# Making the rotations of eight scan steps ahead of the scan and keeping them in DRAM

## The chip, the core and the metric

The kernel runs on one core of one Trainium2 chip. Five engines take part, each with an instruction queue of its own that is worked off in order: TensorE (PE, matrix products), VectorE (DVE), ScalarE (ACT), GpSimd (POOL) and SyncE (SP, which here issues every DMA). Data move between DRAM and the on-chip memory SBUF on sixteen DMA engines. The metric is the device time of one execution in microseconds (us); lower is better.

## What is computed

Two streams (a prompt of 128 tokens and a sample of 1024, width 1024) go through two layers, each a mixer followed by an MLP, all in fp32 accuracy. What matters here is the mixer of layer 0. Three quarters of its channels go through a diagonal state-space scan (S5) in both directions, the rest through a Fourier mixer:

```python
def s5_direction(u, h0_re, h0_im, lam_re, lam_im, log_dt, b_re, b_im, c_re, c_im):
    ab_re, ab_im, bb_re, bb_im = s5_discretize(lam_re, lam_im, log_dt, b_re, b_im)
    bu_re = jnp.einsum("blgh,gph->blgp", u, bb_re)
    bu_im = jnp.einsum("blgh,gph->blgp", u, bb_im)
    ...
    _, _, h_re, h_im = lax.associative_scan(_complex_linear_combine, (a_re, a_im, bu_re, bu_im), axis=1)
    y = jnp.einsum("blgp,ghp->blgh", h_re, c_re) - jnp.einsum("blgp,ghp->blgh", h_im, c_im)
    return y, h_re[:, -1], h_im[:, -1]

def even_mixer(h, ...):
    z = h @ w_in
    ya, s_re, s_im = s5_mixer(z[..., :S5_CH], ...)
    yb = fnet_mixer(z[..., S5_CH:], fnet_w, fnet_b)
    return jnp.concatenate([ya, yb], axis=-1) @ w_out, (s_re, s_im)
```

Each layer also needs six modulation vectors: `silu(cond) @ w_mod + b_mod`, cut in twelve chunks of 512 columns.

## The kernel before

A product in fp32 accuracy is made of three matmuls on split operands (`mm3`, `wh` and `wl` being the high and low part of a weight). A scheduler of the tile framework sets the order of instructions on each engine from a simulated timeline, except in the very first stage, where the order on SP is the order in which the code is written.

**Mixer's products.** The function `layer0_scan` first norms and transposes the tokens and then forms z = h @ w_in in 24 blocks (`z_block`: six blocks of 128 channels, three groups of tokens each). After each second block, from the fourth on, it calls `tables(hb, ...)`, which through `s5_tables` makes the two matrices of one scan step, `et` and `f` (together the tile `ef`), and a small matrix `xd`. A table costs VectorE fourteen operations (L1532 to L1551, L1572), PE some transposes and small products (`pet`, `px`), ScalarE a few copies and GpSimd two sums of 64 columns (`bs` at L1525, `cs` at L1526) and a fill (`bd`, L1555). Tables are kept in SBUF for steps 0 and 1 and stored to DRAM for the others. The list of early steps is 2 to 9, then 0 and 1, ten in all, but the calls come eleven times: the first takes index -1 of the list, so the table of step 1 is made twice. The tables of steps 10 and 11 are made in the scan.

**Scan.** Twelve steps (`hb`), each for 64 channels in both directions. `s5_inputs_of` loads the inputs `u` of a step and makes its rotations `rt`, the powers of a unit complex number for 146 chunks: two complex products of tables of 15 and 9 entries, that is two times L1608, two times L1609 (128 partitions x 540 elements each) and four times L1611 (270 each), on VectorE for step 0 and on GpSimd for all others, and two ScalarE copies (L1613, L1614). `s5_scan` then has eight operations on VectorE: twice `rotated` (two of L1666 on 1168 elements each, with `rt` read), L1669 and L1670, two scans L1673, L1677 and L1678. PE makes its input (`pv`) and output (`py`). Beside the steps nineteen jobs are put: nine of the Fourier mixer ("f") and ten of the modulation ("m"), in the order of the string `JSEQ`. A modulation job loads four pieces of 512 KB (`mst`), has PE multiply them (`pmod`, L127, 16 instructions), and turns the row into columns (`pmc`, `pmg`) with three small VectorE operations (L143 to L146).

**After the scan.** `glu` (products `pg`) follows, then the product with w_out (`mixer_out`), and the MLP's upward half `ff_up` in 16 pairs of weight blocks (`pair`). The ten modulation jobs that the scan did not take are put behind the first ten pairs, one each (`K.late`). Line numbers here are those of the kernel before.

Of the kernel before, what the change touches and what calls it, by code (L numbers as in the profile page):

```python
# [9 lines left out]
F32 = mybir.dt.float32  # L10
# [3 lines left out]
AF = mybir.ActivationFunctionType  # L14
ALU = mybir.AluOpType
# [9 lines left out]
NQ = 48  # L25
SC = 146
UC = 147
YC = 145
EARLY = 10
JSEQ = "ffffmmfffffmmmmmmmm"  # L30
AHA = (3, 7)
TB = 3
RW = 152
# [45 lines left out]
def ap_of(t, off, dims):  # L79

    return bass.AP(tensor=t.tensor, offset=t.offset + off, ap=[list(t.ap[0])] + [list(d) for d in dims])


def load_unit(K, src, n=1024, tags=("wh", "wl")):

    nc = K.nc
    st = stage_tile(K)
    nc.sync.dma_start(st[:, :n], src)
    wh = K.whp.tile([128, 1024], FR, name="wh", tag=tags[0])
    wl = K.wlp.tile([128, 1024], FR, name="wl", tag=tags[1])  # L90
    nc.scalar.activation(wh[:, :n], st[:, :n], AF.Copy)  # L91
    nc.vector.tensor_tensor(wl[:, :n], st[:, :n], wh[:, :n].bitcast(F32), op=ALU.subtract)  # L92
    return wh, wl
# [8 lines left out]
def bank(K, name, tags=None):  # L102

    tags = tags or K.bank_tags
    tag, bufs = tags[K.turn % len(tags)]
    K.turn += 1
    return K.psum.tile([128, 512], F32, name=name, tag=tag, bufs=bufs)
# [132 lines left out]
def mm_cm(K, g, act, w, ps, kbs=range(8)):  # L240

    ah, al = act
    wh, wl = w
    for kb in kbs:
        s = slice(128 * kb, 128 * kb + 128)
        mm3(K.nc, ps[:, :G], wh[:, s], wl[:, s], ah[kb], al[kb], kb == 0, kb == 7)
# [14 lines left out]
def build(tc, A):  # L261
# [6 lines left out]
    with ExitStack() as top:  # L268
# [27 lines left out]
        K.wlp = top.enter_context(tc.tile_pool(name="wlp", bufs=4, reuse_waits="tile"))  # L296
        K.mod = [{}, {}]
        gd, yd = layer0_scan(K)
        K.psum = top.enter_context(tc.tile_pool(name="psum", bufs=1, space=PSUM, reuse_waits="tile"))
        K.bank_tags, K.side_tags = [("s0", 1), ("s1", 1), ("s2", 1)], [("t", 2)]  # L300
# [14 lines left out]
def layer0_scan(K):  # L315

    tc, nc, A = K.tc, K.nc, K.A
    v = nc.vector
    with ExitStack() as ph:
# [10 lines left out]
        with ExitStack() as pa:  # L330
# [86 lines left out]
            s5t = ph.enter_context(tc.tile_pool(name="s5t", bufs=1, reuse_waits="tile"))  # L417
# [3 lines left out]
            S = K.S5  # L421
# [3 lines left out]
            def tables(hb, pool, keep):  # L425
                ef = pool.tile([128, 2176], F32, name="ef", tag="ef", bufs=2 if pool is s5t else 1)
                s5_tables(K, s5t, hb, ef)
                if keep:
                    efs[hb] = ef
                else:  # L430
                    spill[hb] = tc.dram_tile([128, 2176], F32, name=f"ef{hb}")
                    nc.sync.dma_start(spill[hb], ef)

            early = list(range(2, EARLY)) + [0, 1]
            with tc.tile_pool(name="zt", bufs=2, side="right", reuse_waits="tile") as ztp:
                zts = {}
                done = [0]

                def z_block(b, g, w, ps=None):
                    if ps is None:  # L440
                        ps = bank(K, "pz")
                        mm_cm(K, g, acts[g], w, ps)
                    if b >= 6:
                        nc.scalar.activation(zbs[b - 6][:, G * g:G * g + G], ps[:, :G], AF.Copy)
                    else:
                        z_part(b, g, ps)
                    done[0] += 1
                    if done[0] >= 24 - 2 * len(early) and done[0] % 2 == 0:
                        hb = early[(done[0] - 24 + 2 * len(early)) // 2 - 1]
                        tables(hb, s5t, hb < 2)  # L450

                def z_part(b, g, ps):
                    if g == 0:
                        zts[b] = ztp.tile([128, 8 * YC], F32, name="zt", tag="zt")
                        nc.gpsimd.memset(zts[b].rearrange("p (r c) -> p r c", c=YC)[:, :, 128:129], 0.0)
                    zv = zts[b].rearrange("p (r c) -> p r c", c=YC)
                    n = 3 if g < 2 else 2
                    nc.scalar.activation(zv[:, 3 * g:3 * g + n, :128],
                                         ps[:, :128 * n].rearrange("p (r c) -> p r c", c=128), AF.Copy)
                    if g == 2:  # L460
                        nc.scalar.activation(zv[:, :, 129:],
                                             ps[:, 256:384].rearrange("p (r c) -> p r c", c=16), AF.Copy)
                        nc.sync.dma_start(zd[b], zts[b])

                for g in range(3):
                    ps = [bank(K, "pz") for _ in range(4)]
                    for kb in range(8):
                        for wb, p in zip(w, ps):
                            mm_cm(K, g, acts[g], wb, p, (kb,))
                    with tc.high_priority():  # L470
                        for b, p in zip(first, ps):
                            z_block(b, g, None, p)
                for b in range(2, 6):
                    wb = load_unit(K, A["w_in0"][b])
                    for g in range(3):
                        z_block(b, g, wb)
# [3 lines left out]
        with tc.tile_pool(name="s5", bufs=1, side="right", reuse_waits="tile") as s5:  # L480
# [3 lines left out]
                                (1, "sc2", 4, "g_ff_pre"), (1, "sh2", 3, None), (1, "gt2", 5, "g_ff_post")))  # L484
            jobs = [(dft if x == "f" else mods).pop(0) for x in JSEQ]
            K.late = dft + mods
            order = [s5, s5t, s5t]

            def inputs(hb):
                W = s5_inputs_of(K, s5, hb, zd[hb // 2])  # L490
                if hb not in efs:
                    pool = order[(hb + 1) % 3]
                    if hb in spill:
                        efs[hb] = pool.tile([128, 2176], F32, name="ef", tag="ef", bufs=2 if pool is s5t else 1)
                        nc.sync.dma_start(efs[hb], spill[hb])
                    else:
                        tables(hb, pool, True)
                W.m = s5_toeplitz(K, s5, hb)
                W.et, W.f = ef_views(efs[hb])
                return W  # L500
# [1083 lines left out]
def s5_inputs_of(K, pool, hb, zd):  # L1584


    nc, S = K.nc, K.S5
    gp = nc.gpsimd
    q0 = 4 * hb
    e = hb % 2  # L1590
    W = Ctx()

    def T(shape, name, bufs):
        return pool.tile(shape, F32, name=name, tag=name, bufs=bufs)

    W.u = u = T([128, 4, UC], "u", 2)
    gp.memset(u[:, :, 0:1], 0.0)
    gp.memset(u[:, :, 146:147], 0.0)
    for g in range(4):
        r0 = 64 * e + 16 * g  # L1600
        nc.sync.dma_start(u[:, g, 1:146], zd[r0:r0 + 16].rearrange("h (r c) -> r h c", c=YC))
    rt = T([128, 2, 4, RW], "rt", 2)
    t1, t2 = (T([128, 4, 15, 9], n, 1) for n in ("rtmp1", "rtmp2"))
    a = [ap_of(S.rr, 24 * (NQ * ri + q0), [(24, 4), (1, 15), (0, 9)]) for ri in range(2)]
    b = [ap_of(S.rr, 24 * (NQ * ri + q0) + 15, [(24, 4), (0, 15), (1, 9)]) for ri in range(2)]
    eng = nc.vector if hb == 0 else gp
    for ri, op in ((0, ALU.subtract), (1, ALU.add)):
        eng.tensor_tensor(t1, a[0], b[ri], op=ALU.mult)  # L1608
        eng.tensor_tensor(t2, a[1], b[1 - ri], op=ALU.mult)  # L1609
        for d in range(2):  # L1610
            eng.tensor_tensor(ap_of(rt, 4 * RW * ri + d * (2 * RW + 17), [(RW, 2), (9, 15), (1, 9)]),  # L1611
                             t1[:, 2 * d:2 * d + 2], t2[:, 2 * d:2 * d + 2], op=op)
    nc.scalar.activation(rt[:, :, 0:2, 129:146], rt[:, :, 0:2, 0:17], AF.Copy)  # L1613
    nc.scalar.activation(rt[:, :, 2:4, 0:17], rt[:, :, 2:4, 17:34], AF.Copy)  # L1614
    W.R = rt[:, :, :, 0:SC]
    W.rho = rho = T([128, 4, SC], "rho", 1)
    for q in range(4):
        nc.scalar.activation(rho[:, q], K.cst[:, 144 + SC * (q // 2):144 + SC * (q // 2 + 1)], AF.Copy,
                             scale=S.rho[:, q0 + q:q0 + q + 1])
    return W  # L1620


def s5_toeplitz(K, pool, hb):
# [240 lines left out]
```

## Time and profile before

| | us |
|---|---|
| median of 3 runs | 2401.62 (2399.34 to 2403.82) |
| the profiled execution, its own time | 2401.66 |
| its span, first to last instruction | 2399.9 |
| PE busy in the span | 2261.0 (94%) |
| DVE busy | 1695.4 (71%) |
| ACT busy | 980.8 (41%) |
| POOL busy | 190.9 (8%) |

The shares are means over stages that differ. The mixer's products with the tables run from about 84 to 190 us of the span, the scan from 200 to 408, glu and w_out to about 600, the first `ff_up` from about 640 to 1000. All of GpSimd's arithmetic lies before 480. The profiled execution takes 1.8 us outside its span.

### The profile page before, as it was taken

Reading aid. Unit: us, or ns where it says so; the run is one execution under the profiler, and the core shown is the slowest. Engines: PE = TensorE matmul, PEld = TensorE weight load, DVE = VectorE, ACT = ScalarE, POOL = GpSimd, SP = SyncE. Lnnn points to the kernel's source line nnn. Section 1 sums busy time; section 2 is a strip of 40 time slices with the busy share of each in tenths; the row PEclk is TensorE's granted clock in tenths of the full one; section 3 lists DMA queues with packets and bytes.
Section 4 is the critical chain, followed back from the end, with each engine's and each line's share of the span. In section 5 each row is a group of like instructions: output and inputs, shape, how many; then the busy total and the mean of one; then the engine's idle time right before and its main releaser. Section 6 shows DMA issues by size and latency. Waiting matters only on the chain.

```text
span 2399.9 us, 34805 instructions
## 1 busy us (share of the span) xinstructions
PE 2261.0 (94%) x13462; PEld 1974.3 (82%) x13462; DVE 1695.4 (71%) x2694; ACT 980.8 (41%) x1694; POOL 190.9 (8%) x197
## 2 busy tenths in 40 slices
PE   7997676998999999999999899998899999999997
PEld 4996544987888899988888699887899999888886
DVE  7888998747755555757777844867766566677778
ACT  4533324646423233443343452446333333533332
POOL 0127773200000000000000000000000000000000
PEclk9998888999999999999999899998999999999999
DMA  8375675322556553745343431132344446544433
GB/s 308 135 260 170 198 247 154 139 85 91 165 186 204 175 192 123 251 149 157 109 150 98 147 113 36 62 114 79 115 152 129 130 147 219 178 124 137 145 107 141
DMA packets 200453, 361.48 MB, mean 151 GB/s; under 512 B 50064, under 2 KB 95760, under 8 KB 198240
## 3 DMA queue, kind: packets, MB, share of 16 engines
q1 hardware_dynamic: 200288, 359.26, 45.6%
q8 instruction: 106, 1.74, 0.3%
q14 instruction: 59, 0.48, 0.1%
HBM read 256.69 MB, written 102.51 MB: 150 GB/s over the span
## 4 chain that ended last, share of the span: by engine, by line
PE 80%; DVE 13%; DMA 2%; ACT 2%; issue 2%; POOL 1%; SPq 0%; DVEq 0%; ACTq 0%
PE pz L1170 8%; PE pz L1172 8%; PE pz L1173 8%; PE puA L97 6%; PE puA L98 5%; PE puA L99 5%; DVE tp L1666 3%; PE puC L97 3%; PE puC L98 3%; PE puC L99 3%; PE po L256 3%; PE po L257 3%; PE po L258 3%; PE pmod L127 2%; DVE xp L1673 1%
## 5 line engine op out<-in xcount | busy, mean ns | idle before, releaser
L1170 PE MATMUL pz<-wh,hh 128*128 128x512 f32 x840 | 326.2, 389 | 1.2 <-DVE z L1184 1.2
L1173 PE MATMUL pz<-wh,hl 128*128 128x512 f32 x840 | 327.0, 389 | 0.0
L1172 PE MATMUL pz<-wl,hh 128*128 128x512 f32 x840 | 326.9, 389 | 0.0
L1158 ACT ACTIVATE hh<-hr 128x1024 fp32r<-128x1024 f32 x96 | 96.7, 1007 | 262.3 <-PE pz L1172 233.1
L1170 PEld LDWEIGHTS pz<-wh,hh 128*128 128x128 f32 x840 | 157.7, 188 | 34.7 <-issue 2.0
L1173 PEld LDWEIGHTS pz<-wh,hl 128*128 128x128 f32 x840 | 157.7, 188 | 32.7
L1172 PEld LDWEIGHTS pz<-wl,hh 128*128 128x128 f32 x840 | 157.7, 188 | 32.6
L1159 DVE TENSOR_TENSOR hl<-hr,hh 128x1024 fp32r<-128x1024 f32 x96 | 110.9, 1155 | 91.4 <-ACT hh L1158 91.4
L1184 DVE TENSOR_TENSOR z<-z,pz 128x512 f32<-128x512 f32 x192 | 122.8, 681 | 31.8 <-PE pz L1173 31.1
L877 ACT ACTIVATE wh<-c 128x512 fp32r<-128x512 f32 x96 | 60.6, 631 | 186.4 <-DVE c L886 134.3
L933 DVE TENSOR_TENSOR h<-puA,c 128x576 f32<-128x576 f32 (+1 forms) x34 | 24.5, 722 | 155.1 <-PE puA L99 152.0
L257 PE MATMUL po<-wl,act 128*128 128x512 f32 x288 | 113.2, 393 | 0.0
L258 PE MATMUL po<-wh,act 128*128 128x512 f32 x288 | 112.7, 393 | 0.0
L256 PE MATMUL po<-wh,act 128*128 128x512 f32 x288 | 112.3, 395 | 0.0
L878 DVE TENSOR_TENSOR wl<-c,wh 128x512 fp32r<-128x512 f32 x96 | 66.0, 687 | 34.2 <-ACT wh L877 33.8
L877 ACT ACTIVATE wh<-st 128x512 fp32r<-128x512 f32 x96 | 57.1, 627 | 74.8 <-PE puB L98 29.1
L1666 DVE TENSOR_TENSOR tp<-rt,xp 128x1168 f32<-128x1168 f32 x48 | 81.1, 1727 | 7.3 <-ACT xp L1659 6.7
L1134 DVE TENSOR_TENSOR wl<-raw,wh 128x1024 fp32r<-128x1024 f32 (+1 forms) x64 | 73.1, 1153 | 18.2 <-ACT wh L1133 18.2
L92 DVE TENSOR_TENSOR wl<-st,wh 128x1024 fp32r<-128x1024 f32 (+1 forms) x42 | 52.1, 1251 | 47.3 <-ACT wh L91 47.3
L878 DVE TENSOR_TENSOR wl<-st,wh 128x512 fp32r<-128x512 f32 x96 | 63.5, 685 | 29.2 <-ACT wh L877 29.2
L929 ACT ACTIVATE c<-puA 128x576 f32<-128x576 f32 (+1 forms) x68 | 42.2, 621 | 90.0 <-PE puA L99 89.0
L127 PE MATMUL pmod<-mst,csil 128*32 128x512 f32 x384 | 75.9, 659 | 1.0 <-DMA mst<-in_w_mod_dram 1.0
(492 smaller groups left out, 6747.9 us busy)
## 6 DMA issues: line engine op xcount, KB each, us to landing
hr<-hd SPq DMA_DIRECT2D x102, 512.0 KB
mst<-in_w_mod_dram SPq DMA_DIRECT2D x96, 512.0 KB
st<-in_w_ff_dram SPq DMA_DIRECT2D x68, 512.0 KB
hd<-hsum SPq DMA_DIRECT2D x120, 256.0 KB
raw<-in_w_ff_dram SPq DMA_DIRECT2D x56, 512.0 KB
hd<-h SPq DMA_DIRECT2D x98, 256.0 KB
ef<-ef SPq DMA_DIRECT2D x16, 1088.0 KB
xr<-xs SPq DMA_DIRECT2D x32, 512.0 KB
```

The lines of the kernel that those rows point to most:

```text
L97: nc.tensor.matmul(ps, sh, mh, start=start, stop=False, skip_group_check=shared)
L98: nc.tensor.matmul(ps, sh, ml, start=False, stop=False, skip_group_check=shared)
L99: nc.tensor.matmul(ps, sl, mh, start=False, stop=stop, skip_group_check=shared)
L127: nc.tensor.matmul(ps[32 * j:32 * j + 32, :], K.csil[:, kb, :], st[:, 512 * k:512 * k + 512], start=kb < 4, stop=kb >= 4, skip_group_check ...
L256: K.nc.tensor.matmul(ps, ah[kb][:, c], wh[:, s], start=kb == 0, stop=False)
L257: K.nc.tensor.matmul(ps, ah[kb][:, c], wl[:, s], start=False, stop=False)
L258: K.nc.tensor.matmul(ps, al[kb][:, c], wh[:, s], start=False, stop=kb == 7)
L878: v.tensor_tensor(wl, x, wh.bitcast(F32), op=ALU.subtract)
L1170: nc.tensor.matmul(o, hh[:, q, t], wh[:, q], start=start and s == 0 and q == 0, stop=False, skip_group_check=True)
L1172: nc.tensor.matmul(o, hh[:, q, t], wl[:, q], start=False, stop=False, skip_group_check=True)
L1173: nc.tensor.matmul(o, hl[:, q, t], wh[:, q], start=False, stop=s == 1 and q == n - 1, skip_group_check=True)
L1666: v.tensor_tensor(t[:, k], R[:, k:k + 1].to_broadcast([128, 2, 4, SC]), x, op=ALU.mult)
```

## The change

The rotations of steps 0 to 7 (`TURNS = 8`) are made in the stage of the mixer's products, one set after each of the first eight tables, all on GpSimd, into one tile `rt` of a pool with one buffer; ScalarE makes the two copies; SP stores the set to DRAM (`rt0` to `rt7`, 598 KB each, in rows of 584 bytes on the SBUF side). In the scan, `s5_inputs_of` loads the stored set for these steps; for steps 8 to 11 GpSimd makes it there as before. The early list now has eleven steps (2 to 10, then 0 and 1) and the index is mended, so eleven calls make eleven tables; only the table of step 11 is left for the scan. `JSEQ` has three more "m": the scan takes thirteen modulation jobs, and `ff_up` has seven left. The three are both halves of the layer's last gate (`gt2`) and the first half of the next layer's first.

```diff
-EARLY = 10
-JSEQ = "ffffmmfffffmmmmmmmm"
+EARLY = 11
+TURNS = 8
+JSEQ = "ffffmmmfffffmmmmmmmmmm"
...
-            with tc.tile_pool(name="zt", bufs=2, side="right", reuse_waits="tile") as ztp:
+            S.rd = {}
+            with tc.tile_pool(name="zt", bufs=2, side="right", reuse_waits="tile") as ztp, \
+                    tc.tile_pool(name="rtz", bufs=1, side="right", reuse_waits="tile") as rtp:
...
-                    if done[0] >= 24 - 2 * len(early) and done[0] % 2 == 0:
-                        hb = early[(done[0] - 24 + 2 * len(early)) // 2 - 1]
-                        tables(hb, s5t, hb < 2)
+                    n = (done[0] - 24) // 2 + len(early) - 1
+                    if n >= 0 and done[0] % 2 == 0:
+                        tables(early[n], s5t, early[n] < 2)
+                        if n < TURNS:
+                            rt = rtp.tile([128, 2, 4, RW], F32, name="rt", tag="rt")
+                            s5_rotations(K, rt, [rtp.tile([128, 4, 15, 9], F32, name=x, tag=x) for x in ("rt1", "rt2")], n)
+                            S.rd[n] = tc.dram_tile([128, 2, 4, SC], F32, name=f"rt{n}")
+                            nc.sync.dma_start(S.rd[n], rt[:, :, :, 0:SC])
...
-    eng = nc.vector if hb == 0 else gp
-    for ri, op in ((0, ALU.subtract), (1, ALU.add)):
-        eng.tensor_tensor(t1, a[0], b[ri], op=ALU.mult)
...
+    if hb in S.rd:
+        nc.sync.dma_start(rt[:, :, :, 0:SC], S.rd[hb])
+    else:
+        s5_rotations(K, rt, [T([128, 4, 15, 9], n, 1) for n in ("rtmp1", "rtmp2")], hb)
...
+def s5_rotations(K, rt, tmp, hb):
+    nc, S = K.nc, K.S5
+    gp = nc.gpsimd
+    q0 = 4 * hb
+    t1, t2 = tmp
...
+    for ri, op in ((0, ALU.subtract), (1, ALU.add)):
+        gp.tensor_tensor(t1, a[0], b[ri], op=ALU.mult)
+        gp.tensor_tensor(t2, a[1], b[1 - ri], op=ALU.mult)
+        for d in range(2):
+            gp.tensor_tensor(ap_of(rt, 4 * RW * ri + d * (2 * RW + 17), [(RW, 2), (9, 15), (1, 9)]),
+                             t1[:, 2 * d:2 * d + 2], t2[:, 2 * d:2 * d + 2], op=op)
+    nc.scalar.activation(rt[:, :, 0:2, 129:146], rt[:, :, 0:2, 0:17], AF.Copy)
+    nc.scalar.activation(rt[:, :, 2:4, 0:17], rt[:, :, 2:4, 17:34], AF.Copy)
```

What stands in a row on GpSimd, in the stage of the mixer's products, from the second table to the fourth, before the change:

```order
L1525 TENSOR_TENSOR bs<-s5bb 128x64
L1526 TENSOR_TENSOR cs<-s5c 128x64
L1525 TENSOR_TENSOR bs<-s5bb 128x64
L1555 MEMSET bd 128x256
L1526 TENSOR_TENSOR cs<-s5c 128x64
```

And at the same place after it (the lines of the new kernel are eight higher, those of the rotations are 1632, 1633 and 1635):

```order
L1533 TENSOR_TENSOR bs<-s5bb 128x64
L1632 TENSOR_TENSOR rt_980<-s5rr 128x540
L1633 TENSOR_TENSOR rt_981<-s5rr 128x540
L1534 TENSOR_TENSOR cs<-s5c 128x64
L1635 TENSOR_TENSOR rt<-rt_980,rt_981 128x2x135 x2
L1533 TENSOR_TENSOR bs<-s5bb 128x64
L1632 TENSOR_TENSOR rt_1154<-s5rr 128x540
L1633 TENSOR_TENSOR rt_1155<-s5rr 128x540
L1635 TENSOR_TENSOR rt<-rt_1154,rt_1155 128x2x135 x2
L1563 MEMSET bd 128x256
L1534 TENSOR_TENSOR cs<-s5c 128x64
```

The two small sums of each table, which VectorE's operations of the table wait for, now stand between the pieces of a rotation set.

On PE, at the scan's end, the last operations of the last step (`py`) are followed directly by the first product of glu (`pg`) before the change:

```order
L1702 MATMUL py_3930<-s,ef 128x145
L1702 MATMUL py_3931<-s,ef 128x145
L97 MATMUL pg<-gh,wh 128x384 x2
L98 MATMUL pg<-gl,wh 128x384
L99 MATMUL pg<-gh,wl 128x384
```

After it, modulation jobs (`pmod`, then `pmc`, which waits for a ScalarE copy, then `pmg`, which waits for VectorE) stand between them:

```order
L1720 MATMUL py_4012<-s,ef 128x145
L128 MATMUL pmod<-mst,csil 32x512 x2
L142 MATMUL pmc<-cst,mrow 128x128 x4
L158 MATMUL pmg<-cst,mrow 8x128
L128 MATMUL pmod<-mst,csil 32x512 x8
L142 MATMUL pmc<-cst,mrow 128x128 x4
L158 MATMUL pmg<-cst,mrow 8x128
L98 MATMUL pg<-gh,wh 128x384 x2
```

The end of one job and the whole of the last one have moved between the scan's last product and glu's first.

## Rows read from the trace of the kernel before

**Rows 1.** The page, part 4: shares of the chain that ended last, by engine.
```profile
PE 80%; DVE 13%; DMA 2%; ACT 2%; issue 2%; POOL 1%; SPq 0%; DVEq 0%; ACTq 0%
```

**Rows 2.** Busy time in stretches; columns as the first line says, us in a stretch.
```profile
core 0: us, PE busy (x) PEld busy (x) DVE busy (x) ACT busy (x) POOL busy (x), PEclk, DMA share, GB/s
40.00:60.00 20.00, 17.82 (x103) 14.60 (x96) 18.84 (x42) 13.34 (x19) 0.11 (x1) 1.00 0.94 351
84.00:190.00 106.00, 102.21 (x821) 97.11 (x820) 94.90 (x188) 46.65 (x110) 26.01 (x45) 0.97 0.53 183
200.00:397.50 197.50, 144.13 (x1172) 101.15 (x1170) 195.35 (x181) 69.19 (x196) 132.30 (x100) 0.84 0.64 204
700.00:880.00 180.00, 180.00 (x1269) 156.80 (x1269) 98.29 (x163) 53.92 (x91) 0.00 (x0) 1.00 0.58 190
900.00:980.00 80.00, 80.00 (x605) 80.00 (x604) 45.20 (x70) 25.56 (x41) 0.00 (x0) 1.00 0.40 128
```

**Rows 3.** Timeline of DVE beside one whole rotation set: start us, us, instruction, count.
```profile
296.39 0.77 DVE L1677 TENSOR_TENSOR s<-tp 128x584 f32<-128x584 f32 x1
...
298.32 0.68 DVE L555 TENSOR_TENSOR fal<-pab,fah 128x512 fp32r<-128x512 f32 x1
298.92 3.65 DVE L1666 TENSOR_TENSOR tp<-rt,xp 128x1168 f32<-128x1168 f32 x2
...
305.38 4.11 DVE L1673 TENSOR_TENSOR_SCAN xp<-rho,xp 128x584 f32<-128x584 f32 x2
309.52 3.44 DVE L1666 TENSOR_TENSOR tp<-rt,xp 128x1168 f32<-128x1168 f32 x2
```

**Rows 4.** Timeline of POOL in the same stretch, first and last of that set.
```profile
296.52 2.50 POOL L1611 TENSOR_TENSOR rt<-rtmp,rtmp 128x270 f32<-128x270 f32 x2 [2.61 <-DVE tp L1666]
...
308.22 2.23 POOL L1609 TENSOR_TENSOR rtmp<-s5rr 128x540 f32<-128x540 f32 x1
```

**Rows 5.** Timeline of DVE in the last scan step, POOL idle; first and last.
```profile
397.57 2.65 DVE L1666 TENSOR_TENSOR tp<-rt,xp 128x1168 f32<-128x1168 f32 x2
...
407.66 0.76 DVE L1678 TENSOR_TENSOR s<-tp 128x584 f32<-128x584 f32 x1
```

**Rows 6.** Timeline of POOL while DVE waits: half a rotation set.
```profile
194.89 1.18 POOL L1608 TENSOR_TENSOR rtmp<-s5rr 128x540 f32<-128x540 f32 x1
196.03 1.18 POOL L1609 TENSOR_TENSOR rtmp<-s5rr 128x540 f32<-128x540 f32 x1
197.28 1.47 POOL L1611 TENSOR_TENSOR rt<-rtmp,rtmp 128x270 f32<-128x270 f32 x2
```

**Rows 7.** Groups of DVE, 200 to 408.4 us: count | busy us, mean ns | idle before.
```profile
L1666 DVE TENSOR_TENSOR tp<-rt,xp 128x1168 f32<-128x1168 f32 x48 | 81.1, 1727 | 7.3 <-ACT xp L1659 6.7
L1673 DVE TENSOR_TENSOR_SCAN xp<-rho,xp 128x584 f32<-128x584 f32 x24 | 39.3, 1671 | 0.0
L144 DVE TENSOR_TENSOR mc<-mc,vec 128x8 f32<-128x8 f32 x8 | 3.9, 489 | 0.0
```

**Rows 8.** Groups of PE, 700 to 880 us: the modulation's products.
```profile
L127 PE MATMUL pmod<-mst,csil 128*32 128x512 f32 x112 | 24.3, 605 | 0.0
```

**Rows 9.** Groups of DVE, 60 to 192 us: a table's first and last, step 0's rotations.
```profile
L1548 DVE TENSOR_TENSOR ftmp<-s5fe,cs 128x576 f32<-128x576 f32 x12 | 9.8, 820 | 0.9
...
L1572 DVE SCALAR_TENSOR_TENSOR xsb<-cst,s5d,px 64x16 f32<-64x16 f32 x11 | 2.4, 217 | 1.6 <-ACT xsb L1571 1.5
...
L1611 DVE TENSOR_TENSOR rt<-rtmp,rtmp 128x270 f32<-128x270 f32 x4 | 1.5, 422 | 0.0
...
L1608 DVE TENSOR_TENSOR rtmp<-s5rr 128x540 f32<-128x540 f32 x2 | 1.4, 705 | 0.0
```

**Rows 10.** Waits of DVE, 84 to 200 us: total us, times, longest.
```profile
DVE tp L1666 <- ACT xp L1659: 6.2, 1, 6.2
DVE er L1532 <- PE pet L1541: 5.3, 4, 2.8
```

**Rows 11.** Timeline of PE at the scan's end.
```profile
407.80 4.43 PE L1702 MATMUL py<-s,ef 64*128 64x145 f32 x32 [7.31 <-DVE s L1677]
413.75 0.62 PE L97 MATMUL pg<-gh,wh 128*128 128x384 f32 x2 [1.53 <-ACT gh L642]
```

More of the change, by code (lines that the diff above doesn't have):

```diff
@@ L1602, in s5_inputs_of @@
     rt = T([128, 2, 4, RW], "rt", 2)
-    t1, t2 = (T([128, 4, 15, 9], n, 1) for n in ("rtmp1", "rtmp2"))
-    a = [ap_of(S.rr, 24 * (NQ * ri + q0), [(24, 4), (1, 15), (0, 9)]) for ri in range(2)]
-    b = [ap_of(S.rr, 24 * (NQ * ri + q0) + 15, [(24, 4), (0, 15), (1, 9)]) for ri in range(2)]
-    eng = nc.vector if hb == 0 else gp
-    for ri, op in ((0, ALU.subtract), (1, ALU.add)):
-        eng.tensor_tensor(t1, a[0], b[ri], op=ALU.mult)
[L1609 to L1614, printed above, removed]
+    if hb in S.rd:
+        nc.sync.dma_start(rt[:, :, :, 0:SC], S.rd[hb])
+    else:
+        s5_rotations(K, rt, [T([128, 4, 15, 9], n, 1) for n in ("rtmp1", "rtmp2")], hb)
     W.R = rt[:, :, :, 0:SC]
@@ L1620, in s5_inputs_of @@
     return W
+def s5_rotations(K, rt, tmp, hb):
[3 more added lines that the diff above has]
+    t1, t2 = tmp
+    a = [ap_of(S.rr, 24 * (NQ * ri + q0), [(24, 4), (1, 15), (0, 9)]) for ri in range(2)]
+    b = [ap_of(S.rr, 24 * (NQ * ri + q0) + 15, [(24, 4), (0, 15), (1, 9)]) for ri in range(2)]
+    for ri, op in ((0, ALU.subtract), (1, ALU.add)):
[6 more added lines that the diff above has]
+    nc.scalar.activation(rt[:, :, 2:4, 0:17], rt[:, :, 2:4, 17:34], AF.Copy)
 def s5_toeplitz(K, pool, hb):
```

## Prediction, made before the changed kernel was run

> **What bounds the kernel now.** I read the chain that ended last first: it is PE for 80% of the span and DVE for 13% [rows 1]. Then I cut the span into its stages and read who is full in each [rows 2]. From 84 to 190 us (mixer's products and tables) PE is busy for 102.2 of 106 us and DVE for 94.9: two engines near their limit, GpSimd nearly free. From 200 to 397.5 us (the scan) DVE is busy for 195.4 of 197.5 us, PE for 144.1, the DMA engines for 64%: DVE is the bound, and each microsecond taken from it shortens the scan. From 700 to 880 us (`ff_up`) PE is busy for all 180 us.
>
> Then I looked at why a scan step takes DVE so long. The last step runs with GpSimd idle, from 397.57 to 408.42 us, so its operations take 10.85 us [rows 5]. A step beside a whole rotation set, which GpSimd works at from 296.52 to 310.45 [rows 4], runs from 296.39 to 312.96, that is 16.57 us, for the same operations and one `fal` more [rows 3]. `fal` is 0.68 us and overlaps its neighbour by some 0.1, so the clean figure is 11.45 us, and **the rotation set cost DVE 5.1 us**. Pair by pair: two `tp` take 3.65 us here and 2.65 clean [rows 3, 5]. Half a set takes GpSimd 3.83 us when DVE waits, so a whole one 7.66 us [rows 6]. Each engine holds up the other.
>
> **The change part by part.** All sums are against the profiled execution, 2401.66 us (span 2399.9 and 1.8 around it), which is the median of the runs shown, 2401.62, to within 0.1 us.
>
> *Three modulation jobs leave `ff_up`.* From 900 to 980 us, without jobs, PE takes 80.00 / 605 = 0.132 us for one instruction. From 700 to 880 us there are 1269, of which 112 are `pmod` [rows 2, 8] and 27 the transposes of the same seven jobs; the other 1130 should take 149.4 us. The remaining 30.6 us belong to seven jobs: 4.4 us each. Three fewer on a full engine: **-13 us**.
>
> *The scan's DVE.* Between 200 and 397.5 us GpSimd makes ten rotation sets (steps 2 to 11). Afterwards only steps 8 to 11 are made there, and the order puts the first quarter of step 8 ahead of the scan: 3.75 sets. 6.25 sets at 5.1 us: -32. One table less: its eleven groups of DVE operations add up to 7.9 us [rows 9] (first and last of the eleven; each divided by its count of 12 or 11 tables), some 7 without the overlap: -7. Three jobs more: three small operations each, of which the middle one is 0.49 us [rows 7], about 1 us a job: +3. Together -36.
>
> *What comes next in the scan.* The cover that remains is thin in two places. DMA: 12 loads of 512 KB, seven of 598 KB and one table of 1088 KB are 11.6 MB more. At 204 GB/s for a share of 0.64 [rows 2] full engines move 319 GB/s, so this is 36 us on engines that were busy for 126 of 197.5 us: 162 us, in a scan that would last 161. At the best rate in the trace, 351 GB/s at 0.94, it is 31. PE: 144 us at a granted clock of 0.84 plus 13 us of jobs. SP's queue now holds eight rotation loads among those of `u`, `m` and `mst`, and a `pmod` that waits for its load holds up the `pv` and `py` behind it on PE. I take +6 us of new waits on DVE (from 0 to +14; before, it waited 2 us). The scan: **-30 us**.
>
> *The stage of the mixer's products.* Step 0's rotations leave DVE: 1.4 us for L1608, the same for L1609 and 1.5 for L1611 [rows 9]: -4.3. GpSimd gains eight sets. The eighth lies, by the order, beside the scan's start, where DVE waits 6.2 us anyway [rows 10]; seven stand beside tables. No row shows a rotation set beside tables. Below, the price is bounded by 2.8 us a set: over the whole scan `tp` and the scans alone were stretched from 1.33 and 1.32 us to 1.727 and 1.671, by 48 x 0.40 + 24 x 0.35 = 28 us for ten sets [rows 7]. Above, by 7.66 us, the whole length of a set [rows 6]. I take the 5.1 us of the full stretch, since DVE here is 90% busy: +36. Against it, 5.3 us of DVE's idle time are waits for PE's `pet` [rows 10], which go when DVE is the late one; for it, `bs` and `cs` now stand behind pieces of a set on GpSimd, a set's tile has one buffer and waits for its store on SP, and ScalarE's two copies per set hold up what evacuates PE's banks. I let these cancel but for 1 us. **+31 us**.
>
> *The scan's end.* Before, `py` ends at 412.2 and glu's first product starts at 413.75, released by a ScalarE copy [rows 11]. Now one and a half jobs stand between them: some 4.4 us of PE each plus the ways over ScalarE and DVE for `pmc` and `pmg`; in this time the splits for glu get ahead. **+5 us** (0 to +10).
>
> Sum: -13 - 30 + 31 + 5 = -7. The predicted time is 2395 us.
>
> So the work is mostly moved: in the scan 6.25 sets go, in the stage before it seven come. With a price p in both, the two differ by 0.75 p. What is gained is the table, step 0's rotations and the jobs; what decides is the difference of the two prices, times seven.
>
> **The rivals.**
>
> *A. A set costs its whole length beside tables.* Nearly all DVE operations of a table read two operands from SBUF, as `tp` does, and `fal`, which reads one from PSUM, kept its 0.68 us beside a working GpSimd [rows 3]. If no operation of GpSimd finds DVE on such a `fal`, DVE stands still for all 7.66 us: 7 x 2.56 = +18, so 2413 us, slower. It decides from a price of about 6.8 us on, where the time passes 2406. For it: tables are short operations without gaps. Against it: the full stretch in the scan cost 5.1, not 7.66. The Trainium skill has a rule for this (SBUF — State Buffer, "SBUF: two separate sides"): the port pair of the two engines is an exclusive lock, held for a whole instruction, while the other fully blocks. By it alone the price would be the 7.66 us of this rival; the rows agree that both are held up, but show two thirds of it. Chance 25%.
>
> *B. The sets hide.* PE is busy for 102.2 of 106 us in that stage and DVE has 11 us idle; if PE sets the pace and DVE's growth falls mostly into its slack and a price near 2.8, the stage grows by 7 x 2.8 - 4.3 - 5 = 10 us: 2374 us. Against it: 36 us do not fit into 11. Chance 18%.
>
> *C. The scan is held by the DMA engines or PE,* at 14 us of waits and 10 at its end instead of 6 and 5: 2408 us, slower. For it: the 162 of 161 us above. Against it: in this scan DVE waited for nothing so far, and some loads can go ahead in the longer stage before. Chance 12%.
>
> **How the numbers follow.** The forecast, equal prices, 2380 to 2405 us, has 45%. A measurement of this kernel can tell about 0.2%, so "same" is 2397 to 2406. Faster: 32 of the forecast's 45 and B's 18, 0.50. Same: 11 of the forecast, 2 of A and 4 of C, 0.17. Slower: 2 of the forecast, 23 of A and 8 of C, 0.33. The range, 2368 to 2420, takes in B but for its best cases and A but for prices above the bound with waits on top. The likeliest case's own range is 2380 to 2405.
>
> **What would show it.** In the new profile GpSimd's sets should lie between about 85 and 230 us, and DVE's table operations there be stretched, those of 0.75 us to about 1.3. The first `pv` of the scan should come some 30 us later than before. Steps 0 to 7 should have `tp` at 1.33 us, steps 8 to 11 at up to 2.2. The scan should last 175 to 180 us instead of 208, at a DMA share above 0.75. From the last `py` to the first `pg` there should be two jobs. Pairs in `ff_up` should lose 4.4 us three times. I am wrong if DVE waits in the scan for `xp` or `rt`, if it waits beside the tables for `bs` or `cs`, or if the stage of the mixer's products keeps its 106 us.

## The result, and the profile after

The changed kernel takes 2417.06 us (median of 5; 2413.51 to 2423.27) against 2401.62: a ratio of 1.007, with a 95% interval of 1.0057 to 1.0083. It is slower by 15 us, where 7 us of gain were forecast; the time lies inside the stated range, on the other side of the kernel before. The profiled execution has a span of 2415.3 us, 15.4 more than before.

I cut both traces at the same events: the scan's first `pv`, its last `py`, the first `pg` of glu, and the first and last `puA` of the first `ff_up` (all from PE's timeline).

| | before | after | difference | forecast |
|---|---|---|---|---|
| first `pv`, us from the start | 187.6 | 222.0 | +34.4 | +31 |
| scan, first `pv` to last `py` | 224.3 | 211.3 | -13.0 | -30 |
| of it, VectorE busy | 212.3 | 170.8 | -41.4 | -36 |
| of it, VectorE idle | 12.0 | 40.4 | +28.4 | +6 |
| last `py` to first `pg` | 1.9 | 9.9 | +8.0 | +5 |
| first to last `puA` | 423.7 | 409.9 | -13.8 | -13 |

Everything else moves by 0.2 us. One line is far off: VectorE's idle time in the scan. The work left VectorE as planned, and 28 of the 41 us came back as waits.

The stretches of before, then of after, as busy time in stretches (columns as in [rows 2]):

```profile
84.00:187.60 103.60, 99.81 (x804) 95.16 (x802) 92.50 (x181) 45.94 (x107) 23.61 (x43) 0.98 0.53 185
187.60:411.90 224.30, 161.28 (x1304) 115.95 (x1302) 212.28 (x202) 74.31 (x212) 144.54 (x113) 0.83 0.62 196
```

```profile
84.00:222.00 138.00, 108.27 (x810) 101.48 (x809) 132.01 (x176) 48.50 (x120) 98.81 (x103) 0.91 0.64 179
222.00:433.30 211.30, 163.09 (x1305) 112.66 (x1303) 170.84 (x186) 70.56 (x196) 55.30 (x57) 0.85 0.81 256
...
700.00:880.00 180.00, 180.00 (x1292) 164.03 (x1289) 98.37 (x161) 54.80 (x91) 0.00 (x0) 1.00 0.54 174
```

In the stage of the products VectorE is now the full engine (132.0 of 138 us) and PE no longer is. In the scan no engine is full: VectorE 81%, PE 77%, the DMA engines 81%, which were at 62% before. In `ff_up` PE gets through 1292 instructions in the stretch that held 1269 [rows 2].

The operations of a table, groups of VectorE from 84 to 222 us (the 820 ns of [rows 9] are a mean over a longer stretch; cut at the same event, 84 to 187.6 us, it was 755, the first line here): those that read two operands from SBUF are stretched, 755 ns to 1124 for the first; `xsb`, which reads `px` from PSUM, is not.

```profile
L1548 DVE TENSOR_TENSOR ftmp<-s5fe,cs 128x576 f32<-128x576 f32 x11 | 8.3, 755 | 0.8
...
L1556 DVE TENSOR_TENSOR ftmp<-s5fe,cs 128x576 f32<-128x576 f32 x11 | 12.4, 1124 | 0.7
...
L1580 DVE SCALAR_TENSOR_TENSOR xsb<-cst,s5d,px 64x16 f32<-64x16 f32 x10 | 2.2, 216 | 0.8 <-ACT xsb L1579 0.8
```

A scan step with its rotations loaded, VectorE's timeline (answering [rows 3] and [rows 5]): the pair of `tp` is at 2.66 us, as in the clean last step of before, and the whole step is done in 11.3 us. So in this step the contention is gone.

```profile
261.63 2.66 DVE L1684 TENSOR_TENSOR tp<-rt,xp 128x1168 f32<-128x1168 f32 x2
...
272.19 0.76 DVE L1696 TENSOR_TENSOR s<-tp 128x584 f32<-128x584 f32 x1
```

What VectorE waits for in the scan (total us, times, longest; before, the scan's list had 6.7 us for `xp`, 6.2 of them in [rows 10], and 0.8 for `pmc`):

```profile
DVE tp L1684 <- ACT xp L1677: 14.2, 6, 6.9
DVE fal L563 <- DMA m<-xd: 6.3, 1, 6.3
DVE fal L563 <- ACT fah L562: 5.7, 3, 2.4
DVE wl L93 <- DMA out_state_dram<-fin: 4.8, 1, 4.8
DVE mc L144 <- PE pmc L142: 3.5, 4, 1.5
DVE mrow L144 <- PE pmc L142: 3.3, 1, 3.3
```

No single wait explains it: with two of 0.9 and 0.7 us for `fraw` they are eighteen, none above 6.9 us. `xp` and `fah` are copies by ScalarE of what PE made, and PE waits in turn. The chain of work that ended last says for what. In part 4 of the page its shares were PE 80, DVE 13, DMA 2 [rows 1]; now:

```profile
PE 78%; DVE 10%; DMA 6%; ACT 2%; POOL 1%; issue 1%; SPq 0%; DVEq 0%; ACTq 0%; POOLq 0%
```

And these are the transfers on it in the scan (start us, us), 77 us in all; behind 345 us there is none. Before, no transfer stood on the chain in the scan, which from 201 to 377 us went almost only from one VectorE operation to the next.

```profile
223.04 7.06 DMA ef<-ef
230.56 10.59 DMA rt<-rt
242.41 2.37 DMA cd<-in_dft_ch_dram
...
262.41 6.26 DMA u<-zd
...
277.36 6.18 DMA u<-zd
...
292.84 5.70 DMA u<-zd
...
301.92 5.63 DMA mst<-in_w_mod_dram
307.62 6.40 DMA u<-zd
...
317.50 6.77 DMA gd<-yg
324.94 5.02 DMA m<-xd
329.98 8.94 DMA st<-in_w_glu_dram
339.55 5.93 DMA ef<-ef
```

One of them close up. SP's timeline: the four loads of `u` (277.36) stand behind a `mst` load that SP held for 3.26 us, until PE's `pmod` had released a buffer. The second group is PE, whose `pv` waits 2.98 us for that `u`.

```profile
273.34 0.56 SPq L1612 DMA_DIRECT2D rt<-rt  x1
273.99 3.26 SPq L120 DMA_DIRECT2D mst<-in_w_mod_dram  x1
277.36 2.50 SPq L1609 DMA_DIRECT2D u<-zd  x4
```

```profile
283.78 3.02 PE L1671 MATMUL pv<-u,ef 128*64 128x146 f32 x16 [2.98 <-DMA u<-zd]
```

The scan's end on PE (answering [rows 11]): the end of one job and a whole one, with two ways over ScalarE and VectorE each. The whole one and glu's first product:

```profile
436.93 1.92 PE L128 MATMUL pmod<-mst,csil 128*32 128x512 f32 x16
440.27 0.66 PE L142 MATMUL pmc<-cst,mrow 128*128 128x128 f32 x4 [1.42 <-ACT mrow L132]
441.75 0.27 PE L158 MATMUL pmg<-cst,mrow 128*8 128x128 f32 x1 [0.83 <-DVE mrow L147]
443.18 0.62 PE L98 MATMUL pg<-gh,wh 128*128 128x384 f32 x2 [1.15 <-ACT gh L650]
```

### The profile page after: what moved, and what is told of

Read it like the earlier page. It is cut to its first block, busy times and chain, and to the rows that moved or that the text cites. A ratio compares the mean times of both kernels' runs of the same rounds, so it can differ in the third digit from the quotient of the medians.

```text
span 2415.3 us, 34745 instructions
## 1 busy us (share of the span) xinstructions
PE 2258.3 (94%) x13430; PEld 1971.7 (82%) x13430; DVE 1694.4 (70%) x2672; ACT 979.4 (41%) x1687; POOL 176.8 (7%) x202
## 4 chain that ended last, share of the span: by engine, by line
PE 78%; DVE 10%; DMA 6%; ACT 2%; POOL 1%; issue 1%; SPq 0%; DVEq 0%; ACTq 0%; POOLq 0%
PE pz L1178 8%; PE pz L1180 8%; PE pz L1181 8%; PE puA L98 6%; PE puA L100 5%; PE puA L99 5%; PE puC L98 3%; PE puC L100 3%; PE puC L99 3%; PE po L257 2%; PE po L258 2%; PE po L259 2%; PE pmod L128 2%; PE puB L98 1%; PE puB L99 1%
## 5 line engine op out<-in xcount | busy, mean ns | idle before, releaser
L1684 DVE TENSOR_TENSOR tp<-rt,xp 128x1168 f32<-128x1168 f32 x48 | 66.7, 1429 | 14.5 <-ACT xp L1677 14.2
L1142 DVE TENSOR_TENSOR wl<-u,wh 128x1024 fp32r<-128x1024 f32 x64 | 73.8, 1153 | 3.8 <-ACT wh L1141 3.8
```

The costliest lines, as they stand in the source:

```text
L1142: v.tensor_tensor(wl, w, wh.bitcast(F32), op=ALU.subtract)
```

## The experiments

The question is what VectorE's 28 us of new waits are made of. The first theory, "traffic": the loads come late because there are too many of them. Its rivals: "PE" (the three jobs' products), "start" (work that used to run ahead of the scan holds up its beginning), and "chain" (a short step no longer covers the way of a load from the release of its buffer to VectorE, however empty the engines are). For each run the table gives the median, the ratio to the kernel before with its interval, and from its trace the first `pv`, VectorE's idle time and the DMA engines' share in the scan, and when glu begins. One thing holds for all of them: the scheduler orders each version anew, so a run differs from the changed kernel by its edit and by the order of instructions on every engine. No run holds the order fixed.

| run | us | ratio | first `pv` | idle | DMA | first `pg` |
|---|---|---|---|---|---|---|
| before | 2401.6 | | 187.6 | 12.0 | 0.62 | 413.8 |
| after | 2417.1 | 1.007 (1.0057 to 1.0083) | 222.0 | 40.4 | 0.81 | 443.2 |
| jobs_back | 2422.3 | 1.0092 (1.0079 to 1.0105) | 222.9 | 38.6 | 0.77 | 434.6 |
| one_rt_load | 2412.6 | 1.0051 (1.0033 to 1.0069) | 222.5 | 38.2 | 0.78 | 437.0 |
| turns0 | 2398.2 | 0.9992 (0.9981 to 1.0002) | 187.6 | 25.2 | 0.67 | 428.6 |
| turns0_jobs_back | 2399.2 | 0.9994 (0.9985 to 1.0002) | 186.4 | 15.2 | 0.64 | 412.2 |
| thin_loads | 2402.2 | 1.0007 (0.9998 to 1.0015) | 230.2 | 29.8 | 0.56 | 430.4 |
| u3 | 2410.1 | 1.0037 (1.0025 to 1.005) | 220.5 | 38.2 | 0.87 | 433.7 |
| u3_rho2 | 2414.9 | 1.0057 (1.0044 to 1.0071) | 223.2 | 40.5 | 0.84 | 440.0 |
| thin_all | 2393.1 | 0.9965 (0.9953 to 0.9976) | 233.6 | 24.8 | 0.48 | 419.7 |
| turns6 | 2410.0 | 1.0041 (1.0029 to 1.0052) | 216.7 | 35.2 | 0.77 | 438.5 |
| u_gp | 2427.4 | 1.011 (1.0097 to 1.0123) | 236.5 | 50.1 | 0.79 | 456.7 |
| turns0_u3 | 2399.8 | 0.9994 (0.9985 to 1.0003) | 190.4 | 23.7 | 0.68 | 422.8 |
| before_thin | 2405.0 | 1.0012 (1.0003 to 1.0021) | 187.1 | 17.4 | 0.38 | 415.8 |

**The three jobs back in `ff_up`** (jobs_back).

```diff
-JSEQ = "ffffmmmfffffmmmmmmmmmm"
+JSEQ = "ffffmmfffffmmmmmmmm"
```

> The changed kernel with the old JSEQ: the three modulation jobs go back to ff_up, so 6.3 MB of weight loads and some 13 us of PE work leave the scan; the eight early rotation sets stay. ff_up should grow by 13.8 us and the gap between the last py and the first pg shrink from 9.9 to about 2 us. In the changed kernel DVE is idle for 41 us between the first pv and the last py (before: 12). Theory 'traffic' (the DMA engines, busy for 81% there, deliver u, m and ef late): idle falls by about half of the 29 us, to some 27; the whole about 2410. Theory 'PE' (the jobs' own products and their waits for loads hold up pv and py): idle falls to about 18; about 2400. Theory 'start' (loads and products that used to run ahead of the scan now stand at its beginning, whatever the bytes): idle stays at 37 or more; about 2420.

`ff_up` grew by 14.2 us and the gap to glu shrank to 1.9, as expected, but VectorE's idle time stayed at 38.6. So "PE" falls as far as these three jobs go (ten stay in the scan): they and their 6.3 MB are not what VectorE waits for. Here "traffic" fails too, in its simple form of waits in proportion to bytes. By the bounds set down, time and idle time are those of "start"; but only 9.5 us of VectorE's waits in this trace lie in the first two steps. PE's waits for `u` even grew; first the changed kernel, then this run:

```profile
PE pv L1671 <- DMA u<-zd: 12.0, 4, 4.4
```

```profile
PE pv L1671 <- DMA u<-zd: 16.5, 6, 4.3
```

**No early set** (turns0, and turns0_jobs_back with the old `JSEQ` as well).

```diff
-TURNS = 8
+TURNS = 0
```

> The changed kernel with no rotation set made early (all twelve made by GpSimd in the scan), so what is left of the change is the mended list of tables and the three jobs. The stage of the mixer's products should fall from 138 back to about 104 us, if its 34 us are the sets' price on VectorE; if the early tables are what costs, it stays above 110. Scan: before's 224 us less one table (7), plus three jobs (3): 220; ff_up less 13.8; the scan's end 8 longer. Sum 2401.6 - 4 - 7 + 3 + 8 - 14 = 2388. If traffic of the jobs alone makes DVE wait: up to 2398.

> No early rotation set and the old JSEQ: only the mended list of tables is left (eleven tables made once each, the rotations of step 0 on GpSimd instead of VectorE). Against before: one table less in the scan (-7), step 0's rotations off VectorE (-4, or 0 where GpSimd's own 7.7 us at the scan's start take their place). 2391 to 2395. Against the run with the three jobs it tells what these are worth with the scan's DMA engines lightly used: equal times would say that a job costs as much in the scan and at its end as it gave back in ff_up.

The last of these against jobs_back shows the early sets alone, with the same jobs and tables. First the stage of the products and the scan of turns0_jobs_back, then those of jobs_back (columns as in [rows 2]):

```profile
84.00:186.40 102.40, 98.76 (x802) 94.76 (x801) 91.30 (x172) 45.78 (x106) 25.41 (x47) 0.99 0.56 197
...
186.40:410.30 223.90, 159.91 (x1275) 114.14 (x1271) 208.70 (x188) 73.50 (x207) 138.41 (x114) 0.84 0.64 201
```

```profile
84.00:222.90 138.90, 108.09 (x813) 101.14 (x811) 132.41 (x176) 48.63 (x121) 97.36 (x103) 0.93 0.66 178
...
222.90:432.80 209.90, 158.40 (x1272) 110.97 (x1270) 171.27 (x186) 72.06 (x195) 52.20 (x57) 0.84 0.77 239
```

Ahead of the scan VectorE is busy for 132.4 - 91.3 = 41.1 us more, in the scan for 208.7 - 171.3 = 37.4 us less. By GpSimd's timeline the two differ in each stretch by seven sets: when the first `pv` comes, 60 of the rotations' 96 operations are begun in jobs_back and 4 in turns0_jobs_back, and a set has eight. That is 5.9 us a set beside the tables and 5.3 in the scan, so a set costs VectorE nearly the same in both places. But the stage ahead grew by 36.5 us and the scan shrank by only 14.0, since idle time rose from 15.2 to 38.6. **The early sets cost 23 us** (2422.3 - 2399.2), and with the three jobs in the scan 19 (2417.1 - 2398.2).

Without early sets the jobs are worth 1.0 us, inside the noise, where 2388 us had been expected for turns0: `ff_up` gives 12 us and the scan with its end takes as much or more, VectorE's idle time there being 25.2 us against 15.2. (The profiled execution of turns0, 2406.1 us, is the longest of its twelve, so its scan of 233 us is rather too long.) The mended list of tables, alone, is at 0.9994, not told apart from no change either, where 7 to 11 us had been expected: the scan is 0.4 us shorter, VectorE has 3.6 us less to do there and waits 3.2 more.

**Seven of the eight rotation loads left out** (one_rt_load). Steps 1 to 7 use the rotations of step 0.

```diff
-        nc.sync.dma_start(rt[:, :, :, 0:SC], S.rd[hb])
+        if hb == 0:
+            S.kept = T([128, 2, 4, RW], "rtk", 1)
+            nc.sync.dma_start(S.kept[:, :, :, 0:SC], S.rd[hb])
+        rt = S.kept
```

> The changed kernel, but the stored rotation set is loaded for step 0 alone and steps 1 to 7 use that one (so seven loads of 598 KB, 4.2 MB, are left out, and the rotations of these steps are those of step 0); all else stays, the eight sets are still made and stored. Traffic: DVE's 41 us of idle time fall by 4.2/11 of the 29 us, to about 30, total about 2406. If the rotation loads hold up SP's queue more than their bytes say (many short rows): down to 20, about 2396. PE or start: idle stays at 38 or more, 2414 or more.

4.5 us less, with an interval that overlaps that of the changed kernel; VectorE's idle time fell by 2. By the bounds set down, the idle time is that of "PE or start", and the time lies between these and "traffic". The rotation loads alone are not it.

**Thin loads for the jobs of the scan** (thin_loads), which leave about 26 MB out; the changed kernel moved 54 in its scan (256 GB/s for 211 us).

```diff
-        nc.sync.dma_start(st[:, :1024], K.A[f"w_mod{layer}"][ch, :, h])
+        nc.sync.dma_start(st[:, :32], K.A[f"w_mod{layer}"][ch, :, h, 0:32])
...
-                                 st[:, 512 * k:512 * k + 512],
+                                 ap_of(st, 0, [(0, 16), (1, 32)]),
```

> The changed kernel, but the thirteen modulation jobs of the scan load 32 of each 1024 columns and have PE multiply these over and over (same products in number and size; the modulation's values are other ones): some 26 MB of loads leave the scan. Theory 'traffic' (the sum of all loads fills the engines and the eight loads that SP keeps under way): the share falls from 0.81 to about 0.45 and DVE's 40.5 us of idle time to 20 or less; 2395 or less. Theory 'chain' (a step of 11.5 us no longer covers the way from the release of u's buffer over GpSimd, SP, the load, PE and ScalarE to VectorE, however empty the engines): idle stays at 32 or more, 2408 or more.

2402.2: 15 us less than the changed kernel. "Traffic" had asked for 2395 and 20 us of idle time, "chain" for 2408 and 32; measured are 29.8. Neither fits whole. The scan:

```profile
230.20:426.90 196.70, 154.57 (x1331) 108.67 (x1328) 166.83 (x190) 73.36 (x198) 45.23 (x52) 0.89 0.56 155
```

From 250 us to the scan's last step VectorE's waits add up to 24.6 us in the changed kernel and to 12.5 here, and PE's waits for `u` fall from 12.0 to 3.8 us. The rest lies at the two ends: here, one wait of 10.6 us for the first `xp`, and 5.6 at the last splits. The profiled execution is 13 us shorter than the changed kernel's: the scan by 14.6, the way from the last `py` to the first `pg` by 6.4, while the first `pv` comes 8.2 us later. So the new order shows in the sum, too.

**A third buffer for `u`** (u3), and **a second for `rho`** on top (u3_rho2).

```diff
-    W.u = u = T([128, 4, UC], "u", 2)
+    W.u = u = T([128, 4, UC], "u", 3)
```

> The changed kernel with a third buffer for u, so that a step's u can be loaded a step earlier. In the changed kernel PE waits 12.0 us for u's loads in the scan. Chain: these waits go and DVE's 40.5 us of idle time fall by about 8 to 12; 2407. Traffic: an earlier issue meets the same full engines; idle falls by 3 or less, 2414 or more.

> As the one before, with a second buffer for rho too: ScalarE's copies of rho for the next step then needn't wait for VectorE's two scans of this one (17.8 us of ScalarE's waits in the changed kernel), and what stands behind them on ScalarE (xp, fah) comes earlier. Chain: idle falls by 5 more than with u alone, 2402. If ScalarE's wait for rho hides nothing that VectorE needs: the same as with u alone, within 2 us.

The buffer brought 7 us, nearer to what "chain" had asked (2407), but not by its mechanism: VectorE's idle time in the scan fell by 2 us only, which "traffic" had asked, and the DMA share rose to 0.87. PE's waits for `u` went from 12.0 to 6.4 us and those for `ef` from 6.5 to 15.2. The chain of this run can be followed back to 302.5 us only; the transfers on it there are others:

```profile
302.53 8.19 DMA rt<-rt
...
315.98 8.71 DMA rt<-rt
...
326.31 7.34 DMA mst<-in_w_mod_dram
...
333.71 7.80 DMA mst<-in_w_mod_dram
```

So when one load comes earlier, the next is the late one; that fits a shared limit better than a single late buffer. The second buffer for `rho` gave nothing, or cost 5 us, outside both expectations; why stays open.

**All three cuts together** (thin_all: thin loads, one rotation load, third `u`).

> The changed kernel with three cuts together: the scan's jobs load 32 of 1024 columns (the modulation's values are other ones), the stored rotation set is loaded for step 0 alone and used by steps 1 to 7 (their rotations are wrong), and u has a third buffer. What DVE's idle time is without the traffic: 'traffic' in full gives 15 or less (scan 182, about 2388); 'chain and order' (the way PE, ScalarE, VectorE of a step, and the scan's beginning) gives 25 or more (scan 192 or more, 2398 or more). With the thin loads alone idle was 29.8.

2393.1, that is 24 us below the changed kernel and about the sum of the three alone (15, 4.5 and 7). The scan's length is what "traffic" had asked, the idle time of 24.8 us nearly what "chain and order" had:

```profile
233.60:416.10 182.50, 150.78 (x1328) 106.81 (x1328) 157.61 (x184) 70.34 (x192) 34.70 (x44) 0.90 0.48 140
```

From 250 us to the last step VectorE waits for 8.0 us (24.6 in the changed kernel, 12.5 with thin loads alone); the other 17 lie at the beginning, 10.8 of them before two `fal` (their waits are 8.1 and 6.3 us, and the first begins 3.6 us before this cut), and at the end, 4.9 before the last splits. The first `pv` is released by a load of `u` that stands on the chain for 8.05 us just ahead of the cut (from 225.49 us), so the beginning is still late. In the scan itself only two transfers are left on the chain:

```profile
329.13 5.64 DMA yd<-fy
...
400.79 2.33 DMA gd<-yg
```

**The thin loads in the kernel before** (before_thin; the same edit) are the control.

> The kernel before with the cut of the thin loads: the ten modulation jobs of its scan load 32 of each 1024 columns (other values of the modulation; PE's products as many and as large). Some 20 MB of loads leave the scan. If the loads became the limit only by the change, as 'traffic' has it, nothing is to be had here, since VectorE waits for 12 us in all: 2398 to 2402. If thin loads shorten any scan of this kernel by the 15 us that they took from the changed one: about 2387, and the loads would not explain the loss.

Not faster, if anything 3 us slower, though 20 MB are gone and the DMA share fell to 0.38:

```profile
187.10:413.90 226.80, 160.58 (x1304) 115.00 (x1302) 209.48 (x204) 74.20 (x212) 141.41 (x112) 0.85 0.38 112
```

In the kernel before, neither VectorE's waits in the scan nor the longer ones of PE are for a load; in the changed kernel the same edit is worth 15 us. So **the loads became late by the change**. This holds for about half of VectorE's new idle time: with all three cuts 24.8 us of 40.4 stay, against 12.0 before. And since the edit changes the order of instructions in both kernels, the 15 us are not all shown to be bytes.

**Six early sets** (turns6: `TURNS = 6`).

> The changed kernel with six early sets instead of eight: in the changed kernel the store of the eighth set stands on SP's queue ahead of m, u and cd of the first steps, since GpSimd ends that set only at 229 us. The stage of the mixer's products loses two sets (34.4 / 8 each): the first pv at about 213; VectorE gets two sets more in the scan (4.6 each: +9). Theory 'start' (the late sets and their stores hold up the scan's beginning, 11.3 us of idle in the first two steps): these fall to about 5 and the total to 2410 or less. Otherwise the sets only move: 2417 less 2 or 3 for waits that two longer steps cover, 2414.

2410.0, as "start" asked. The time alone doesn't tell, since two eighths of the 23 us would be 5.8. But VectorE's waits in the first two steps are 0.8, 0.2 and 1.6 us in place of 3.7, 6.3 and 1.3, and its idle time in the scan falls from 40.4 to 35.2. So part of the loss is the beginning, some 5 us of it in idle time: in the changed kernel GpSimd ends the eighth set at 229.3 us, and on SP its store (230.56, 10.59 us on the chain above) stands ahead of loads of `m`, `u` and `cd` for the first steps; one of `u` was held for 4.3 us until that store had landed.

**`u` loaded from GpSimd's queue** (u_gp).

```diff
-        nc.sync.dma_start(u[:, g, 1:146], zd[r0:r0 + 16].rearrange("h (r c) -> r h c", c=YC))
+        nc.gpsimd.dma_start(u[:, g, 1:146], zd[r0:r0 + 16].rearrange("h (r c) -> r h c", c=YC))
```

> The changed kernel with the loads of u issued by GpSimd right behind its fills of u, instead of SP, whose queue runs in order and keeps eight transfers under way. If SP's queue is what makes u late (12.0 us of PE's waits in the scan, in the changed kernel), these waits go and the whole falls by 8 or more, to 2409 or less. If it is the transfers themselves, or if GpSimd's issuing costs VectorE as its arithmetic does: no gain or a loss, 2416 or more.

2427.4, the slowest. On GpSimd's timeline the issues themselves stop for 5 us at a time, and what stands behind them is the last table's `cs`:

```profile
222.10 0.59 POOL L1609 DMA_DIRECT2D u<-zd  x1 [5.29 <-issue]
...
229.69 1.17 POOL L1609 DMA_DIRECT2D u<-zd  x2 [5.05 <-issue]
...
235.57 0.31 POOL L1534 TENSOR_TENSOR cs<-s5c 128x64 f32<-128x64 f32 x1
```

VectorE waits 13.9 us for that `cs`. So the run moves a wait and does not tell whether SP's order alone makes `u` late. The Trainium skill (DMA: Bandwidth & Descriptors, "Issuing engines are not separate DMA queues") says that transfers issued by different engines run on the same sixteen DMA engines and save only the issuing time; the trace agrees, in so far as the sixteen engines are busy for 171 us of the scan in both (0.79 x 216.4 and 0.81 x 211.3).

**The third buffer without early sets** (turns0_u3).

> No early set, the three jobs, and a third buffer for u: whether the scan with rotations in it, where the run without the buffer had 25 us of idle time on VectorE, gains from it as well. If so about 2392; if PE and not u was late there (its waits for u's loads were under 1 us): 2398, the same as without.

No gain: 2399.8 against 2398.2. Where PE doesn't wait for `u`, the buffer is worth nothing. No version that leaves nothing out is shown to be faster than the kernel before.

## Why the prediction was wrong

**Modulation jobs out of `ff_up`: right.** -13 forecast, -13.8 measured.

**The price of a set: nearly right.** 5.1 us in both places was the forecast's hinge; measured are 5.9 beside the tables and 5.3 in the scan, and the difference, times seven, is about 4 us of the loss. The stage of the products grew by 34.4 us (+31 forecast), and the slack named there, 5.3 us of waits for `pet`, was used up (0.4 left). Rival A, which decides from a price of about 6.8 us, fell; so did B, whose stage was to grow by 10 us. The exclusive lock of the Trainium skill (SBUF — State Buffer, "SBUF: two separate sides") would make it, by an estimate from [rows 6], 7.66 us a set, the whole length of each instruction; here the runs show about three quarters of that beside the tables (5.9).

**VectorE's work in the scan: right.** -36 forecast, -41.4 measured. **The scan's end: right in kind,** +8.0 for +5.

**The new waits in the scan: wrong, and this is the step that failed.** "I take +6 us of new waits on DVE (from 0 to +14)"; measured +28.4. The load of the DMA engines was well counted: with the cuts used here the forecast's 36 us come on top of 0.62 x 224.3 = 139, and 0.81 x 211.3 = 171 were measured. What failed is what I made of it. I held 162 us against a scan of 161 and charged little more than the excess, as if engines at their limit cost nothing until the sum is longer than the scan. But each load has its own moment. At a share of 0.81 the four pieces of `u`, 290 KB, stand on the chain for 5.7 to 6.4 us, and they can't be issued before their buffer is free and SP's queue has come to them. I read the rest so: a step of 16.6 us covered that, a step of 11.3 does not. PE's waits for `u` in the scan bear it out: they are not among its longer waits in the kernel before and in turns0, whose steps are long, and they come to 16.5 us in jobs_back and 11.5 in one_rt_load, whose steps are short though they load less than the changed kernel. By the landing records of the traces the four pieces take long where nobody waits for them, too: a median of 6.4 us from the first issue to the last landing in the kernel before and 8.4 in turns0, against 7.7 in the changed kernel. The argument that VectorE "waited for nothing so far" was no evidence: it waited for nothing because it was itself the late one, at a DMA share of 0.62.

**Rival C came nearest,** with 12% of chance. It named late loads and the direction, and its 14 and 10 us were to give 2408; they were 28 and 8. Part of the 28 was in nobody's list: the eighth set's store on SP ahead of the first steps' loads; the experiment with six sets puts the scan's beginning, with what else changes then, at 5 us of idle time. That the time lies inside the stated range at all is luck: the range reached to 2420 for the sake of rival A, whose price did not come.

**The signs listed** behind the prediction split accordingly: the first `pv` 34 us later, `tp` at 1.33 us in steps with loaded rotations, a share above 0.75 and jobs between `py` and `pg` all came; a scan of 175 to 180 us did not come, and VectorE waits for `xp`, which stood there as what would make it wrong. Of the two others that stood there, the stage of the products did not keep its 106 us, and beside the tables VectorE has no listed wait for `bs` or `cs`.

**Open.** Three jobs fewer left the idle time where it was, thirteen thin ones halved its middle part, so it doesn't go by bytes alone. How much is transfer time, and how much SP's order, stays open. All of SP's transfers share eight completion semaphores in turn, so that each is issued only when the eighth before it has landed; and SP waits in the changed scan both for transfers to end and for buffers,

```profile
SPq L1727 <- DMA mst<-in_w_mod_dram: 10.6, 15, 1.1
SPq L1727 <- ACT yg L1723: 10.5, 3, 6.7
SPq L120 <- PE pmod L128: 9.3, 5, 3.3
SPq L1609 <- DMA ef<-ef: 6.7, 4, 2.9
```

and the one run that took `u` off this queue brought a wait of its own. How much the new order of instructions adds in each run is not shown, either.

## What to carry to other kernels

Work that is moved off a full engine into a neighbouring stage at the same price per piece is no gain by itself: here the stage that received it grew by 36.5 us, and the stage that lost it shrank by 14.0, down to its next limit. Before counting the second as won, look at every load that the long steps had covered, and charge waits well before the transfers' sum reaches the stage's length: here 28 us at a share of 0.81. Whether loads are the new limit is cheap to ask: thin them out in both versions. Here the changed one gained 15 us and the old one nothing. If the order of instructions is made anew each time, look at where in the scan the time was gained before calling it bytes.

## What the runs showed of the hardware that I had not expected

That a rotation set on GpSimd costs VectorE 5 to 6 us beside the shorter operations of the tables (5.9) as beside those of the scan (5.3): a table's operation of 755 ns went to 1124 here, as `tp` had gone from 1.33 us to 1.73 in the scan of before. That GpSimd, when it issues transfers itself, can stand for 5 us between two of them (5.29 and 5.05 in u_gp), and with it all that is queued behind. And that PE's mean granted clock in the stage of the products, which lies between its two levels of 1.2 and 2.4 GHz, went from 0.98 to 0.91 where PE came to wait: it was idle for 29.7 of 138 us (3.8 of 103.6 before) and busy for 108.3 us where 99.8 had done, with 810 instructions for 804.
